# Operand preparation, product order and row ends in the late half of an encoder block

## The chip, the cores and the metric

The kernel runs on one core of one Trainium2 chip. The metric is the time of one execution on the device in microseconds. The kernel before was timed three times: 2582.22, 2582.96 and 2584.04 us, median 2582.96. One further execution was recorded by the profiler.

The core has five engines with a queue each: TensorE (PE) multiplies matrices, VectorE (DVE) and ScalarE (ACT) work elementwise, GpSimd (POOL) does little here, and SyncE (SP) issues all DMAs of this kernel, in order.

## The reference

One layer over 2048 positions of 1024 features: a mixing part (two head groups), a feed-forward part with a causal convolution, and a last norm. The part around the change is the feed-forward of the second half of the positions:

```python
def conv_ffn(h, w_up, w_conv, b_conv, w_down):
    a = h @ w_up
    C = a.shape[-1]
    a = lax.conv_general_dilated(
        a, w_conv[:, None, :].astype(a.dtype), window_strides=(1,),
        padding=[(CONV_W - 1, 0)], dimension_numbers=('NWC', 'WIO', 'NWC'),
        feature_group_count=C) + b_conv.astype(a.dtype)
    g, val = jnp.split(a, 2, axis=-1)
    return (jax.nn.silu(g) * val) @ w_down
...
        x = x + jnp.concatenate([out_a, out_b], axis=-1) @ w_out[l]
        x = x + conv_ffn(rms_norm(x, norm_ffn_g[l]), w_up[l], w_conv[l], b_conv[l], w_down[l])
    return rms_norm(x, norm_final_g)
```

`D_MODEL` is 1024, `D_FF` 2816, `CONV_W` 3. Inputs and output are float32.

## The kernel before

Every float32 product is made of three matmuls with operands in a rounded format: each operand is split into a high part (a copy by ScalarE that rounds) and a low part (the difference, by VectorE), and high x high, high x low and low x high are summed. The helper `both` (L911) makes such a pair. So every operand costs one ScalarE and one VectorE operation before TensorE can use it.

The kernel is one stream of instructions in which a planner, at build time, gives every engine its order by its own estimate of times; the order in the source is a priority, not the order of execution. Tiles come from pools; a tile has a name, and `BUFS` (L39) says how many buffers each name has. A new tile waits until an old one in its place has been read for the last time. When one pool is closed and another opened, the new tiles lie where the old ones lay.

The first half of the positions (1024) goes through mixing, up projection, convolution and down projection in other functions, which the change doesn't touch. The second half goes through `late_half` (L960):

- `c_late` (L922) ends the mixing part. It leaves rows in DRAM (`rows_d`) and normed, transposed rows in the tiles `yf`.
- **Up projection.** The 1024 rows and the 2 x 2816 columns are handled by a scheme with seven products for eight (Strassen's, in Winograd's form). The rows' operands are called Y: P1 and P2 use quarters of the rows as they are (y11, y21), P3 to P7 use sums and differences (Y22, T4, T1, T2, T3), which `first` (L983) and the lines after it build with VectorE. The columns are done in 22 chunks (`NF`) of 128 gate and 128 value columns. For each chunk f, `up_raw` (L1034) loads two weight tiles `rawl` (gate and value, 512 KB each), `up_gate` (L1041) splits the gate part for P1 and P2 (tiles xgP1, xgP2), and `up_sums` (L1047) makes and splits the five sums for P3 to P7 (tiles sf, xs). One product is 12 matmuls (`prod`, L1011), into a PSUM bank A, B or C.
- `up_step(f)` (L1067) does a chunk: it first computes P1 of the chunk f + 1 into a bank A and copies it to a tile `pc` (`kept`, L1029); adds C of f and its kept P1 into `cv` (L1081); then P6 on top of P1 (kept as u2), P7 (kept as p7), P5 on top of A, sums with p7 (L1086), P4 on top of B, sum with u2 (L1087), P3 on top of A, and copies A (L1089). Then P2 of f + 1 into a bank C, the sums of f + 1, the loads and the gate split of f + 2. The convolution, the gate and the store to `act_d[f]` follow (L1099 to L1112). A chunk of 2 x 1024 values is in `cv` (2 buffers) until its gate is formed.
- **Down projection** (`down_half`, L1114). For two blocks b of 512 rows, and for 22 chunks f of the inner dimension: load a chunk of the weights (`rawl`) and of `act_d` (`df`), split both (dh, dl, ah, al, 5 buffers each), and do 24 matmuls for four row tiles t and two column halves, accumulating in 8 PSUM banks D. The last four chunks go row by row instead (L1166): all four for t = 0, then its end, and so on. `end` (L1140) adds the row to what `rows_d` holds, squares it (the squares go to a tile that is called `df` as well), forms the norm factor by a power on GpSimd, scales and stores the row.

All DMAs are issued by SP, each in its turn: a store that waits for its data holds the loads behind it.

Of the kernel before, what the change touches and what calls it, by code (L numbers as in the profile page):

```python
# [18 lines left out]
P = 128  # L19
S = 2048  # L20
D = 1024
KC = D // P
DFF = 2816
NF = DFF // P
HALF = 1024
TB = 512
EPS = 1e-6
# [9 lines left out]


BUFS = {  # L39
    "raw": 2, "rawl": 4, "whi": 4, "wlo": 4, "thi": 1, "tlo": 1, "acc": 8,  # L40
# [7 lines left out]
}  # L48


# [4 lines left out]
class Block:  # L55
# [904 lines left out]
    def late_half(self, accp, close_c):  # L960
        nc, tc = self.nc, self.tc
        self.c_late(accp)
        close_c()
        kw = dict(bufs=1, reuse_waits="tile")
        es = ExitStack()
        self.rawp = self.ctx.enter_context(tc.tile_pool(name="rawlate", **kw))
        xp = self.xp = es.enter_context(tc.tile_pool(name="xpool", **kw))
        yp = es.enter_context(tc.tile_pool(name="y2pool", **kw))
        self.up = es.enter_context(tc.tile_pool(name="upool", **kw))
        self.upp = es.enter_context(tc.tile_pool(name="ups", space=PSUM, **kw))  # L970
        self.w_up = self.a["w_up"][0].rearrange("(c p) n -> p c n", p=P)
        self.X, self.ps, self.p1 = {}, {}, {}
# [36 lines left out]
        self.down_half(1)  # L1009
# [21 lines left out]
        self.nc.scalar.activation(t, ps, AF.Copy)  # L1031
        return t

    def up_raw(self, f):  # L1034
        self.raw = getattr(self, "raw", {})
        for c, c0 in ((0, f * P), (1, DFF + f * P)):
            t = self.til(self.rawp, [P, 1024], F32, "rawl")
            self.dma(t.rearrange("p (a b) -> p a b", b=P), self.w_up[:, :, c0:c0 + P])
            self.raw[f, c] = t

    def up_gate(self, f):  # L1041
        g = self.raw[f, 0]
# [21 lines left out]
        for n in S:  # L1064
            self.X[f, n] = S[n]

    def up_step(self, f):  # L1067

        nc = self.nc
        tt = nc.vector.tensor_tensor  # L1070
        if f:
            if f + 1 < NF:
                p1 = self.prod(f + 1, "P1", "A")
                self.p1[f + 1] = self.kept(p1)
        else:
            for i in range(2):
                self.p1[i] = self.kept(self.ps[i, "A"])
        a = self.til(self.fp, [P, 2, HALF + 2], F32, "cv")
        nc.scalar.activation(a[:, :, 0:2], self.halo[:, f:f + NF + 1:NF, :], AF.Copy)
        lo, hi = slice(2, 2 + TB), slice(2 + TB, 2 + HALF)  # L1080
        tt(a[:, 0, lo], self.ps.pop((f, "C")), self.p1.pop(f), op=ALU.add)  # L1081
        A = self.prod(f, "P6", "A")
# [6 lines left out]
        nc.scalar.activation(a[:, 0, hi], A, AF.Copy)  # L1089
        for k in ("A", "B"):  # L1090
            self.ps.pop((f, k))
        if f and f + 1 < NF:
            self.prod(f + 1, "P2", "C")
        if f + 1 < NF:
            self.up_sums(f + 1)
        if f + 2 < NF:
            self.up_raw(f + 2)
            self.up_gate(f + 2)
# [15 lines left out]
    def down_half(self, half):  # L1114

        nc, tc = self.nc, self.tc
        w_down = self.a["w_down"][0].rearrange("(f p) n -> p f n", p=P)
        with ExitStack() as es:
            kw = dict(bufs=1, reuse_waits="tile")
            dp = es.enter_context(tc.tile_pool(name="downp", **kw))  # L1120
            pp = es.enter_context(tc.tile_pool(name="downs", space=PSUM, **kw))
            gf = dp.tile([P, D], F32, name="gf")
            self.dma(gf, self.a["norm_final_g"].unsqueeze(0).broadcast_to([P, D]))
            for b in range(2):
                bank = {}
                parts = []

                def mms(f, t):
                    w, x = parts[f]
                    ts = slice(t * P, (t + 1) * P)  # L1130
                    for col in range(2):
                        cs = slice(col * 512, (col + 1) * 512)
                        if f == 0:
                            bank[t, col] = self.til(pp, [P, TB], F32, "D")
                        ps = bank[t, col]
                        for i, j in ((0, 0), (0, 1), (1, 0)):
                            nc.tensor.matmul(ps, lhsT=x[i][:, ts], rhs=w[j][:, cs], start=f == 0 and i + j == 0,  # L1137
                                             stop=f == NF - 1 and i == 1)

                def end(t):  # L1140
                    i = 4 * b + t
                    x = self.til(dp, [P, D], F32, "xo")
                    self.dma(x, self.rows_d[i])
                    for col in range(2):
                        cs = slice(col * 512, (col + 1) * 512)
                        nc.vector.tensor_tensor(x[:, cs], bank[t, col], x[:, cs], op=ALU.add)
                    junk = self.til(dp, [P, D], BF16, "df")
                    r = self.row_scale(self.fp, x, junk)
                    nc.vector.scalar_tensor_tensor(x, x, r, gf, op0=ALU.mult, op1=ALU.mult)
                    t0 = half * HALF + i * P  # L1150
                    self.dma(self.out[0, t0:t0 + P, :], x)

                for f in range(NF):
                    raw = self.til(self.rawp, [P, 1024], F32, "rawl")
                    self.dma(raw, w_down[:, f, :])
                    w = [self.til(dp, [P, 1024], F32R, "dh"), self.til(dp, [P, 1024], F32R, "dl")]
                    self.both(w, raw)
                    xf = self.til(dp, [P, TB], F32, "df")
                    self.dma(xf, self.act_d[f][:, b * TB:(b + 1) * TB])
                    x = [self.til(dp, [P, TB], F32R, "ah"), self.til(dp, [P, TB], F32R, "al")]  # L1160
                    self.both(x, xf)
                    parts.append((w, x))
                    if f < NF - 4:
                        for t in range(4):
                            mms(f, t)
                for t in range(4):  # L1166
                    for f in range(NF - 4, NF):
                        mms(f, t)
                    end(t)

    def run(self):
        tc = self.tc
# [50 lines left out]
```

## Time and profile before

| | us |
|---|---|
| median of three runs | 2582.96 |
| the profiled execution, its own time | 2580.12 |
| its span, on which all positions below lie | 2578.3 |
| up projection of the late half, first matmul | 1872.4 |
| its last product ends | 2310.4 |
| down projection, first matmul | 2316.5 |
| its first block ends | 2439.3 |
| its second block begins | 2449.3 |
| its last matmul ends | 2570.6 |

The profile gives each engine's busy time. TensorE's records are pipelined, so its busy time overstates it a little: a matmul of 0.39 us follows its predecessor by 0.23 us. A row of the timeline reads: start, length, engine, line, operation, output tile <- input tiles, shapes, count, and in brackets the idle time just before and who ended it. A row of the waits reads: who waited, for whom, us in total, times, longest. L72 is the line through which every DMA is issued, L913 and L914 are the two operations of `both`; for these the tile's name tells what is meant.

### The profile page before, as it was taken

The page shows a single profiled execution, that of the slowest core. Times are in us where ns is not written, and L with a number is a line of the kernel's source. Part 1 is how long each engine was busy: PE and PEld are TensorE (multiplying, and loading weights), DVE is VectorE, ACT ScalarE, POOL GpSimd, SP SyncE. Part 2 cuts the span into 40 slices and gives each one's busy share as a digit, 9 for nine tenths or more (in the row PEclk, how much of TensorE's full clock was granted, in tenths as well). Part 3 has the DMA queues.
Part 4 walks back from the last instruction along what each step waited for, and adds up shares of the span by engine and source line. Part 5 has one row for each costly group of instructions (what it writes and reads, how often), then busy time and mean ns, then how long its engine had stood idle before and what let it go on. Part 6 is the DMA issues. An engine that isn't in the chain of part 4 may idle for free.

```text
span 2578.3 us, 32600 instructions
## 1 busy us (share of the span) xinstructions
PE 2503.3 (97%) x11346; PEld 2048.2 (79%) x11346; DVE 1707.3 (66%) x2981; ACT 1269.4 (49%) x2376; POOL 291.3 (11%) x314
## 2 busy tenths in 40 slices
PE   8999999999999999999999999999989999999898
PEld 5787777878788888888888888887868888878687
DVE  5237676565458777777776777766388888884433
ACT  4337687554356555554545554553345455453332
POOL 3204131000112001001100100112100000000000
PEclk9999999999999999999999999999999999999999
DMA  6863524666733233323332323356413222236452
GB/s 185 256 164 92 176 90 142 171 187 210 263 120 119 88 105 112 97 87 105 108 101 87 106 93 91 110 174 228 155 49 97 75 89 82 81 112 209 158 170 71
DMA packets 314880, 336.27 MB, mean 130 GB/s; under 512 B 49596, under 2 KB 218756, under 8 KB 314700
## 3 DMA queue, kind: packets, MB, share of 16 engines
q1 hardware_dynamic: 314716, 334.19, 42.3%
q8 instruction: 90, 1.47, 0.2%
q14 instruction: 74, 0.61, 0.1%
HBM read 267.80 MB, written 66.46 MB: 130 GB/s over the span
## 4 chain that ended last, share of the span: by engine, by line
PE 85%; DMA 4%; DVE 4%; ACT 3%; issue 2%; POOL 1%; SPq 0%; POOLq 0%; ACTq 0%; DVEq 0%
PE mm L174 12%; PE mm L172 12%; PE mm L176 12%; PE D L1137 9%; PE dn L172 3%; PE dn L174 3%; PE dn L176 3%; PE A L1026 3%; PE A L1025 3%; PE A L1024 3%; PE s L656 2%; PE s L716 2%; PE o L705 2%; PE s L655 2%; PE s L717 2%; PE o L704 2%
## 5 line engine op out<-in xcount | busy, mean ns | idle before, releaser
L172 PE MATMUL mm<-thi,whi 128*128 128x512 f32 x960 | 376.3, 392 | 1.9 <-DVE vn L381 1.9
L174 PE MATMUL mm<-tlo,whi 128*128 128x512 f32 x960 | 376.6, 392 | 0.0
L176 PE MATMUL mm<-thi,wlo 128*128 128x512 f32 x960 | 376.3, 392 | 0.2 <-DVE wlo L126 0.2
L664 ACT ACTIVATE s<-s,part 128x512 f32<-128x512 f32 (+3 forms) x320 | 190.6, 596 | 214.0 <-DVE part L659 138.4
L728 DVE TENSOR_TENSOR pl<-e,ph 128x512 fp32r<-128x512 f32 (+1 forms) x320 | 204.7, 644 | 111.4 <-PE o L705 67.3
L172 PE MATMUL mm<-whi,thi 128*128 128x512 f32 x640 | 253.9, 399 | 7.2 <-POOL whi L114 5.5
L174 PE MATMUL mm<-wlo,thi 128*128 128x512 f32 x640 | 254.5, 398 | 3.1 <-DVE wlo L126 3.0
L176 PE MATMUL mm<-whi,tlo 128*128 128x512 f32 x640 | 252.8, 395 | 0.0
L722 ACT ACTIVATE e<-s 128x512 f32<-128x512 f32 (+1 forms) x320 | 166.6, 531 | 174.6 <-PE s L717 84.2
L727 ACT ACTIVATE ph<-e 128x512 fp32r<-128x512 f32 (+1 forms) x320 | 179.2, 567 | 131.9 <-PE o L704 118.0
L114 POOL TENSOR_SCALAR whi<-raw 128x1024 fp32r<-128x1024 f32 x130 | 149.1, 1149 | 796.8 <-PE mm L176 184.5
L172 PEld LDWEIGHTS mm<-thi,whi 128*128 128x128 f32 x960 | 180.4, 188 | 40.4 <-DVE vn L381 2.5
L174 PEld LDWEIGHTS mm<-tlo,whi 128*128 128x128 f32 x960 | 180.5, 188 | 37.8
L176 PEld LDWEIGHTS mm<-thi,wlo 128*128 128x128 f32 x960 | 180.4, 188 | 37.7 <-DVE wlo L126 0.7
L126 DVE TENSOR_TENSOR wlo<-raw,whi 128x1024 fp32r<-128x1024 f32 x130 | 163.8, 1262 | 60.5 <-POOL whi L114 60.4
L659 DVE TENSOR_REDUCE part<-s 128x1 f32<-128x512 f32 x192 | 127.9, 684 | 46.4 <-PE s L656 45.4
L1137 PE MATMUL D<-dh,ah 128*128 128x512 f32 x352 | 139.8, 397 | 16.0 <-ACT ah L913 16.0
L850 DVE TENSOR_TENSOR acc<-dn,acc 128x512 f32<-128x512 f32 x176 | 120.7, 686 | 52.0 <-PE dn L176 51.0
L172 PEld LDWEIGHTS mm<-whi,thi 128*128 128x128 f32 x640 | 120.9, 189 | 32.7 <-POOL whi L114 7.0
L174 PEld LDWEIGHTS mm<-wlo,thi 128*128 128x128 f32 x640 | 121.5, 190 | 29.6 <-DVE wlo L126 6.6
L176 PEld LDWEIGHTS mm<-whi,tlo 128*128 128x128 f32 x640 | 121.3, 190 | 24.0
L1137 PE MATMUL D<-dl,ah 128*128 128x512 f32 x352 | 139.3, 396 | 0.0
(295 smaller groups left out, 5506.2 us busy)
## 6 DMA issues: line engine op xcount, KB each, us to landing
m<-kx SPq DMA_DIRECT2D x160, 256.0 KB
raw<-in_w_up_dram SPq DMA_DIRECT2D x44, 512.0 KB
rawl<-in_w_up_dram SPq DMA_DIRECT2D x44, 512.0 KB
rawl<-in_w_down_dram SPq DMA_DIRECT2D x44, 512.0 KB
m<-kx SPq DMA_DIRECT2D x160, 136.0 KB
raw<-in_w_in_dram SPq DMA_DIRECT2D x40, 512.0 KB
v<-vd SPq DMA_DIRECT2D x80, 256.0 KB
x<-in_x_dram SPq DMA_DIRECT2D x24, 512.0 KB
```

Source lines behind the costliest of these rows:

```text
L114: self.cast_ins = self.nc.gpsimd.tensor_scalar(out, in_, 1.0, 0.0, ALU.mult, ALU.add).ins
L126: nc.vector.tensor_tensor(lo, raw, f32(hi), op=ALU.subtract)
L172: mm(ps, lhsT=ah[k], rhs=bh[k], start=k == 0, stop=False)
L174: mm(ps, lhsT=ah[k], rhs=bl[k], start=False, stop=False)
L176: mm(ps, lhsT=al[k], rhs=bh[k], start=False, stop=k == n - 1)
L659: nc.vector.tensor_reduce(dst, ps, axis=AX.X, op=ALU.min)
L664: nc.scalar.activation(ps[:, :n], ps[:, :n], AF.Exp, scale=-1.0, bias=dst, accum_out=ls[:, tt, sb:sb + 1])
L722: nc.scalar.activation(e[:, c], ps[:, c], AF.Exp, scale=-1.0)
L727: nc.scalar.activation(ph[:, c], e[:, c], AF.Copy)
L728: nc.vector.tensor_tensor(pl[:, c], e[:, c], f32(ph[:, c]), op=ALU.subtract)
L850: nc.vector.tensor_tensor(ac, ps, ac, op=ALU.add)
L1137: nc.tensor.matmul(ps, lhsT=x[i][:, ts], rhs=w[j][:, cs], start=f == 0 and i + j == 0, stop=f == NF - 1 and i == 1)
```

## The change

The change touches the late half only. In the up projection:

- Weight tiles: three `rawl` buffers instead of four. Gate and value parts are loaded by separate calls.
- P1 and P2 run two chunks ahead instead of one. Chunks 0, 1 and 2 have theirs emitted before the steps; the gate splits of 0 and 1 come before the sums of chunk 0, that of 2 before the transforms of the rows (`first`). xgP1 has two buffers, bank B one instead of two, bank C three instead of two.
- `up_step` is cut in `up_mms` (products) and `up_conv` (convolution, gate, store). The convolution of the last chunk is emitted after the first two preparations of the down projection.

In the down projection:

- The 44 chunks of both blocks are numbered through. `prep(n)` makes the operands of one; `ready(n + 2)` is called ahead of chunk n's matmuls, and `ready(n + 4 + max(0, t - 1))` ahead of the row tile t in the last four chunks, so chunks 0 and 1 of the second block are prepared within the last rows of the first. The operands have seven buffers.
- A row ends in two column halves: the eight times three matmuls are ordered by half, and each half is added, squared (into its own tile `jk`), scaled and stored on its own; the two sums of squares are added by one more small operation.

```diff
-    "raw": 2, "rawl": 4, "whi": 4, "wlo": 4, "thi": 1, "tlo": 1, "acc": 8,
+    "raw": 2, "rawl": 3, "whi": 4, "wlo": 4, "thi": 1, "tlo": 1, "acc": 8,
...
-    "xgP1l": 1, "xgP1h": 1,   "pc": 3, "A": 3, "B": 2, "C": 2,
-    "dh": 5, "dl": 5, "df": 3, "ah": 5, "al": 5, "xo": 4, "D": 8,
+    "xgP1l": 2, "xgP1h": 2,   "pc": 3, "A": 3, "B": 1, "C": 3,
+    "dh": 7, "dl": 7, "df": 3, "ah": 7, "al": 7, "xo": 4, "jk": 2, "s2": 2, "D": 8,
...
-        self.up_raw(0)
+        for c in range(2):
+            self.up_raw(0, c)
         self.up_gate(0)
+        self.up_gate(1)
         self.prod(0, "P1", "A")
         self.prod(0, "P2", "C")
         self.up_sums(0)
+        self.up_raw(1, 1)
+        self.up_gate(2)
...
         first(slice(384, 512))
-        self.up_raw(1)
-        self.up_gate(1)
         self.prod(1, "P1", "A")
         self.prod(1, "P2", "C")
         self.both(T3, y12)
...
         self.both(T4, y21)
+        self.prod(2, "P1", "A")
+        self.prod(2, "P2", "C")
         for f in range(NF):
-            self.up_step(f)
+            self.up_mms(f)
+            if f + 1 < NF:
+                self.up_conv(f)
         es.close()
...
+    def up_mms(self, f):
...
+        n = f + 2
+        if f == 0:
+            for i in range(3):
                 self.p1[i] = self.kept(self.ps[i, "A"])
+        elif n < NF:
+            self.p1[n] = self.kept(self.prod(n, "P1", "A"))
...
+        if f and n < NF:
+            self.prod(n, "P2", "C")
         if f + 1 < NF:
             self.up_sums(f + 1)
         if f + 2 < NF:
+            self.up_raw(f + 2, 1)
+        if f + 3 < NF:
+            self.up_gate(f + 3)
...
+            def prep(n):
+                b, f = divmod(n, NF)
+                raw = self.til(self.rawp, [P, 1024], F32, "rawl")
+                self.dma(raw, w_down[:, f, :])
+                w = [self.til(dp, [P, 1024], F32R, "dh"), self.til(dp, [P, 1024], F32R, "dl")]
+                self.both(w, raw)
+                xf = self.til(dp, [P, TB], F32, "df")
+                self.dma(xf, self.act_d[f][:, b * TB:(b + 1) * TB])
+                x = [self.til(dp, [P, TB], F32R, "ah"), self.til(dp, [P, TB], F32R, "al")]
+                self.both(x, xf)
+                parts[n] = w, x
...
+            def ready(n):
+                while len(parts) <= min(n, 2 * NF - 1):
+                    prep(len(parts))
+
+            ready(1)
+            self.up_conv(NF - 1)
             for b in range(2):
                 bank = {}
+                rows = []
+                for n in range(b * NF, (b + 1) * NF - 4):
+                    ready(n + 2)
+                    for t in range(4):
+                        mms(bank, n, t)
+                for t in range(4):
+                    ready(n + 4 + max(0, t - 1))
                     i = 4 * b + t
                     x = self.til(dp, [P, D], F32, "xo")
                     self.dma(x, self.rows_d[i])
+                    ss = self.til(dp, [P, 2], F32, "s2")
+                    jk = self.til(dp, [P, D], BF16, "jk")
                     for col in range(2):
                         cs = slice(col * 512, (col + 1) * 512)
+                        for m in range(n + 1, n + 5):
+                            mms(bank, m, t, (col,))
                         nc.vector.tensor_tensor(x[:, cs], bank[t, col], x[:, cs], op=ALU.add)
+                        nc.scalar.activation(jk[:, cs], x[:, cs], AF.Square, accum_out=ss[:, col:col + 1])
+                    rs = self.til(dp, [P, 1], F32, "rs")
+                    nc.vector.tensor_tensor(rs, ss[:, 0:1], ss[:, 1:2], op=ALU.add)
+                    nc.vector.tensor_scalar(rs, rs, 1.0 / D, EPS, ALU.mult, ALU.add)
+                    r = self.til(dp, [P, 1], F32, "rstd")
+                    nc.gpsimd.tensor_tensor(r, rs, self.mhalf[:, 0:1], op=ALU.pow)
                     t0 = half * HALF + i * P
+                    for col in range(2):
+                        cs = slice(col * 512, (col + 1) * 512)
+                        nc.vector.scalar_tensor_tensor(x[:, cs], x[:, cs], r, gf[:, cs], op0=ALU.mult, op1=ALU.mult)
+                        self.dma(self.out[0, t0:t0 + P, cs], x[:, cs])
```

The `BUFS` lines are shortened to the names that change or are spoken of. `mms` is the old function of that name with the column half as an argument.

More of the change, by code (lines that the diff above doesn't have):

```diff
@@ L971, in late_half @@
         self.w_up = self.a["w_up"][0].rearrange("(c p) n -> p c n", p=P)
-        self.X, self.ps, self.p1 = {}, {}, {}
+        self.X, self.ps, self.p1, self.raw = {}, {}, {}, {}
         (y11, y21), (y12, y22) = self.yf
@@ L1032, in kept, with up_raw @@
         return t
[L1034 to L1039, printed above, removed]
+    def up_raw(self, f, c):
+        t = self.raw[f, c] = self.til(self.rawp, [P, 1024], F32, "rawl")
+        c0 = c * DFF + f * P
+        self.dma(t.rearrange("p (a b) -> p a b", b=P), self.w_up[:, :, c0:c0 + P])
     def up_gate(self, f):
+        if f:
+            self.up_raw(f, 0)
         g = self.raw[f, 0]
@@ L1065, in up_sums @@
             self.X[f, n] = S[n]
-    def up_step(self, f):
+    def up_mms(self, f):
         nc = self.nc
         tt = nc.vector.tensor_tensor
[L1071 to L1076, printed above, removed]
+        n = f + 2
+        if f == 0:
+            for i in range(3):
                 self.p1[i] = self.kept(self.ps[i, "A"])
-        a = self.til(self.fp, [P, 2, HALF + 2], F32, "cv")
+        elif n < NF:
+            self.p1[n] = self.kept(self.prod(n, "P1", "A"))
+        a = self.cv = self.til(self.fp, [P, 2, HALF + 2], F32, "cv")
         nc.scalar.activation(a[:, :, 0:2], self.halo[:, f:f + NF + 1:NF, :], AF.Copy)
@@ L1091, in up_step @@
             self.ps.pop((f, k))
-        if f and f + 1 < NF:
-            self.prod(f + 1, "P2", "C")
+        if f and n < NF:
+            self.prod(n, "P2", "C")
         if f + 1 < NF:
@@ L1096, in up_step, with up_conv @@
         if f + 2 < NF:
-            self.up_raw(f + 2)
-            self.up_gate(f + 2)
+            self.up_raw(f + 2, 1)
+        if f + 3 < NF:
+            self.up_gate(f + 3)
+    def up_conv(self, f):
+        nc = self.nc
+        tt = nc.vector.tensor_tensor
+        a = self.cv
         t = self.til(self.fp, [P, 2, HALF], F32, "ts")
@@ L1123, in down_half @@
             self.dma(gf, self.a["norm_final_g"].unsqueeze(0).broadcast_to([P, D]))
+            parts = {}
+            def prep(n):
[9 more added lines that the diff above has]
+                parts[n] = w, x
@@ new lines, in mms @@
+            def mms(bank, n, t, cols=(0, 1)):
+                w, x = parts[n]
+                f = n % NF
+                ts = slice(t * P, (t + 1) * P)
+                for col in cols:
+                    cs = slice(col * 512, (col + 1) * 512)
+                    if f == 0:
+                        bank[t, col] = self.til(pp, [P, TB], F32, "D")
+                    for i, j in ((0, 0), (0, 1), (1, 0)):
+                        nc.tensor.matmul(bank[t, col], lhsT=x[i][:, ts], rhs=w[j][:, cs], start=f == 0 and i + j == 0,
+                                         stop=f == NF - 1 and i == 1)
@@ L1124, in down_half @@
+            def ready(n):
[3 more added lines that the diff above has]
+            self.up_conv(NF - 1)
             for b in range(2):
                 bank = {}
[L1126 to L1138, printed above, removed]
@@ L1140, in end @@
-                def end(t):
+                rows = []
[5 more added lines that the diff above has]
+                    ready(n + 4 + max(0, t - 1))
                     i = 4 * b + t
@@ L1148, in end @@
-                    r = self.row_scale(self.fp, x, junk)
-                    nc.vector.scalar_tensor_tensor(x, x, r, gf, op0=ALU.mult, op1=ALU.mult)
-                    t0 = half * HALF + i * P
[L1151 to L1169, printed above, removed]
+                        nc.scalar.activation(jk[:, cs], x[:, cs], AF.Square, accum_out=ss[:, col:col + 1])
[3 more added lines that the diff above has]
+                    r = self.til(dp, [P, 1], F32, "rstd")
```

2 lines of the change are left out of this document (1 added, 1 removed), and 2 rows, old and new, of the table BUFS.

## The prediction

> **What bounds the kernel now.** The page comes first, then a table by stage of the part that the change touches (the list of stages, with busy time and granted clock), then the waits of TensorE in that part.
>
> ```profile
> span 2578.3 us, 32600 instructions
> PE 2503.3 (97%) x11346; PEld 2048.2 (79%) x11346; DVE 1707.3 (66%) x2981; ACT 1269.4 (49%) x2376; POOL 291.3 (11%) x314
> ...
> 1872.40:1923.70 51.30, 42.69 (x171) 33.41 (x170) 43.98 (x53) 23.96 (x33) 0.93 (x1) 0.90 0.15 42
> 1923.70:2310.40 386.70, 386.70 (x1690) 316.41 (x1688) 326.74 (x400) 197.12 (x299) 0.00 (x0) 1.00 0.25 82
> 2310.40:2316.50 6.10, 0.01 (x1) 0.00 (x0) 6.06 (x6) 6.03 (x7) 0.00 (x0) 0.66 0.93 300
> 2316.50:2439.30 122.80, 122.77 (x528) 101.08 (x528) 52.89 (x60) 39.02 (x50) 1.65 (x3) 0.98 0.53 179
> 2439.30:2449.30 10.00, 0.08 (x2) 0.04 (x1) 5.94 (x8) 2.83 (x4) 0.55 (x1) 0.64 0.94 322
> 2449.30:2570.60 121.30, 121.30 (x528) 100.04 (x528) 45.05 (x52) 32.99 (x44) 1.65 (x3) 0.99 0.37 121
> 2570.60:2578.30 7.70, 0.04 (x1) 0.00 (x0) 2.21 (x4) 1.15 (x2) 0.55 (x1) 0.80 0.27 112
> ...
> PE D L1137 <- ACT ah L913: 16.0, 2, 9.9
> PE A L1026 <- DVE xgP1l L914: 4.1, 1, 4.1
> PE B L1025 <- DVE t3l L914: 3.9, 1, 3.9
> ...
> 2569.57 0.39 PE L1137 MATMUL D<-dh,al 128*128 128x512 f32 x1
> ...
> 2570.25 0.39 PE L1137 MATMUL D<-dh,al 128*128 128x512 f32 x1
> ```
>
> The columns of a stage are its length, busy time of PE, PEld, DVE, ACT and POOL with counts, the granted clock, the DMA share and GB/s. TensorE bounds the kernel: nothing but fewer or shorter holes in it pays. The last two rows lie three matmuls apart, 0.68 us, so one takes 0.2267 us. That prices the holes:
>
> - Entry of the up projection (1872.4 to 1923.7). Its 171 records are 163 products' matmuls, 37.0 us, and two sets of short transposes, about 1.2. So 51.3 less 38.2, 13.1 us, is lost.
> - The steady up projection (next row) has no hole.
> - Entry of the down projection: 6.1 us of nothing, and 122.8 us for 528 matmuls that need 119.7. So 6.1 + 3.1 = 9.2 us. The extra is a reduced clock: 0.66 granted in the hole.
> - The border of the two row blocks: 10.0 us, then 121.3 for 119.7, together 11.6.
> - The tail: 7.7 us behind the last matmul.
>
> The change has 41.6 us before it, 1.6% of the span; it adds no matmul and takes none away.
>
> **Part 1: three product pairs first (entry of up).** Who is late here is read from the timelines of VectorE and ScalarE.
>
> ```profile
> 1883.07 0.68 DVE L914 TENSOR_TENSOR xgP1l<-rawl,xgP1h 128x512 fp32r<-128x512 f32 x1
> ...
> 1888.71 0.69 DVE L914 TENSOR_TENSOR xgP1l<-rawl,xgP1h 128x512 fp32r<-128x512 f32 x1 [1.95 <-ACT xgP1h L913]
> ...
> 1897.22 2.28 DVE L914 TENSOR_TENSOR t3l<-cv,t3h 128x2048 fp32r<-128x2048 f32 x1
> ...
> 1905.70 0.68 DVE L914 TENSOR_TENSOR t2l<-cv,t2h 128x512 fp32r<-128x512 f32 x1
> ...
> 1888.05 0.63 ACT L913 ACTIVATE xgP1h<-rawl 128x512 fp32r<-128x512 f32 x1 [8.83 <-PE A L1025]
> ```
>
> VectorE is busy 43.98 of 51.3 us here and its early part is nearly solid: it makes T3 (ready 1899.5) and T2 (ready 1906.4), without which P7 and P6 of step 0 cannot run. TensorE's first wait, 4.1 us, is for the low part of chunk 1's gate weights, at 1883.07. The chain then turns on itself: xgP1 has one buffer, so ScalarE sits 8.83 us until TensorE has read it, and VectorE 1.95 us behind ScalarE. The new order makes the gate parts of chunks 0 and 1 at once, with two xgP1 buffers, and all six leading products (72 matmuls, 16.3 us) can run before T3. That moves one product, 2.7 us, into the time that is lost anyway, and takes VectorE's 1.95 us of idle out of the way of T3 and T2. Against it stand chunk 2's two splits (2 x 0.68 on VectorE) ahead of T3, and the fact that P2 of chunk 2 no longer fills the wait for T2.
>
> If T3 and T2 come no earlier, step 0 ends where it does, and I bound the part at a loss of 0.5 us; if they come 3 us earlier, at a gain of 5. I take +2.5, near the idle that goes. The 13.1 us are thus mostly kept: they are VectorE's.
>
> **Part 2: the steady steps.** Weight buffers (rawl 4 to 3), one B bank for two, and P1 and P2 two chunks ahead change the ring of every step. Nothing is gained (no hole), so the question is what it costs.
>
> ```profile
> 2089.93 0.58 ACT L1089 ACTIVATE cv<-A 128x512 f32<-128x512 f32 x1
> ...
> 2098.91 0.21 ACT L1079 ACTIVATE cv<-halo 128x4 f32<-128x4 f32 x1 [1.29 <-DVE ts L1110]
> ...
> 2118.15 0.21 ACT L1079 ACTIVATE cv<-halo 128x4 f32<-128x4 f32 x1 [1.29 <-DVE ts L1110]
> ...
> 2100.05 0.69 DVE L1081 TENSOR_TENSOR cv<-C,pc 128x512 f32<-128x512 f32 x1
> ```
>
> A step takes 19.24 us (the two halo copies). The tightest new ring is pc, which keeps three buffers: P1's copies of two coming steps and u2 hold all three, so p7's copy now waits until L1081 of the following step has used its own P1 copy. That needs a cv buffer, free when the step before has been convolved. In the rows: from L1089 (2089.93) to the end of L1081 (2100.74) 10.8 us; then p7's copy 0.6 (as L1089), L1086 0.7 (as L1081), twelve matmuls of P3 2.7, and about 0.6 for hand-overs (an estimate from the 0.1 to 0.3 between neighbouring rows): 15.4 us a turn against 19.24. The other four products and the two early ones fill the waiting. The weight loads have one buffer less, but P1 and P2 of a chunk can stand anywhere in their step. I take 0, from +1 down to -15 if the ring bites.
>
> **Part 3: entry of down, conv of the last chunk put behind two preparations.**
>
> ```profile
> 2300.79 0.58 ACT L1089 ACTIVATE cv<-A 128x512 f32<-128x512 f32 x1
> ...
> 2309.58 0.33 SPq L72 DMA_DIRECT2D act<-ts  x1
> 2309.96 0.42 SPq L72 DMA_DIRECT2D gf<-in_norm_final_g_dram  x1
> 2310.45 0.60 ACT L1089 ACTIVATE cv<-A 128x512 f32<-128x512 f32 x1 [0.75 <-PE A L1026]
> 2310.47 1.71 SPq L72 DMA_DIRECT2D df<-act  x3
> 2310.94 1.99 ACT L913 ACTIVATE dh<-rawl 128x1024 fp32r<-128x1024 f32 x2
> ...
> 2315.86 1.29 ACT L913 ACTIVATE ah<-df 128x512 fp32r<-128x512 f32 x2
> ```
>
> ScalarE was idle 0.75 us ahead of 2310.45 and yet no dh was made before: the weights' parts stand behind the last L1089 in its queue, as if the pool of the down projection opens only there. Its first ah comes after four dh copies (4 x 1.05) and a conv operation. On SP, the df loads stand behind the store of chunk 20, which waits for that chunk's convolution: 0.83 us before the end of the last product. DMA then runs at 300 GB/s with a share of 0.93, so the first df cannot land much earlier than it is issued.
>
> The edit keeps the place of the pool, so the late dh stays. It shortens the queue ahead of ah (two preparations, three weight buffers) by one or two dh, 1.05 to 2.1 us, and the conv operation, 1.2. And chunk 20's store may come earlier against the end: the last two steps now have no P1 or P2 to run, five products of 12 (13.6 us) against the 9.66 us between the two L1089, if they are not interleaved as now. I take 2.0 us of the 9.2: lower bound 0 (the landing decides), upper 9.2 (all ready at the end, and no slow matmul). The conv behind the two preparations costs nothing beside TensorE's 10.9 us for chunks 0 and 1; its store is read only with the last chunk of block 0.
>
> **Part 4: the border.**
>
> ```profile
> 2442.42 1.78 SPq L72 DMA_DIRECT2D df<-act  x3
> ...
> 2448.58 0.63 ACT L913 ACTIVATE ah<-df 128x512 fp32r<-128x512 f32 x1 [4.72 <-DMA df<-act]
> ...
> 2449.26 0.79 PE L1137 MATMUL D<-dh,ah 128*128 128x512 f32 x1 [9.92 <-ACT ah L913]
> ```
>
> Here the cause is plain. The last four chunks hold four of five operand buffers, and the squares of the row ends use df's three, so the next block's df loads are issued 3.1 us after TensorE stopped and land in a burst (322 GB/s, share 0.94). With seven buffers, squares in tiles of their own, and chunks 22 and 23 prepared beside rows 2 and 3 of block 0, these loads have 10.9 us of matmuls above them. Work beside them: two preparations take VectorE 2 x (1.22 + 0.69) = 3.8 us, two row ends about 3.0 each, 9.8 of 10.9 us; it just fits, and is spread as the chunks may be made earlier. So the whole 11.6 us less a little: +11.4, down to +6 if df is still late by a part of the burst.
>
> **Part 5: rows in two parts (tail).** From the timelines at the end and SP's waits:
>
> ```profile
> 2571.46 1.06 ACT L137 ACTIVATE df<-xo 128x1024 bf16<-128x1024 f32 x1 [4.29 <-DVE xo L1146]
> ...
> 2573.46 1.28 DVE L1149 SCALAR_TENSOR_TENSOR xo<-xo,rstd,gf 128x1024 f32<-128x1024 f32 x1 [0.66 <-POOL rstd L141]
> ...
> SPq L1219 <- DMA out_dram<-xo: 2.1, 1, 2.1
> ```
>
> Behind the last matmul a half square replaces the whole: 1.06 less about 0.6 (a 128x512 operation, as L1089), 0.45 gained; one more small addition costs 0.15 to 0.2. The two halves of the last product take as long as the whole, but the first half is stored 0.65 us sooner, and the last store is 256 KB. At 300 GB/s that is 0.87 us less to move. I take 0.6 of it, bounds 0 and 0.9. So +0.9 (0.3 to 1.4).
>
> The Trainium skill, "DMA: Bandwidth & Descriptors", section "Anatomy of one DMA", speaks against this: some 2.0 us of a DMA is fixed, mostly the write's receipt, and only the rest scales with bytes. By it nearly all of the 2.1 us above would stay, and the sum would be 0.4 us smaller; no row here has a store of 256 KB alone to tell.
>
> **Sum:** 2.5 + 0 + 2.0 + 11.4 + 0.9 = 16.8 us. The profiled execution took 2580.1 us, 1.8 around its span; the median of the runs shown is 2582.96. As a difference it carries over: 2583.0 - 16.8 = **2566 us**.
>
> **Rivals.**
>
> *The entry of down closes too.* If df and dh of the first two chunks are made before the last product ends (their old neighbours in memory are read early in that step), all 9.2 us go, 7.2 more than in my sum: **2559**. For it: df's loads need only stand ahead of or right behind chunk 20's store. Against it: the late dh. Here the Trainium skill, "TensorE: Matmul & The Clock Gate", section "Part 1: The HAM clock gate", gives a half-way case: an idle window of about 3.4 us halves the clock. By it a hole cut from 6.1 to under 3.4 us would also save the 3.1 us of slow matmuls, one of 4.1 us would not; the trace agrees so far as waits of 3.9 us and more are followed by slow ones.
>
> *The border keeps a part.* The loads of chunks 22 and 23, output stores and residual rows share one SP queue in order; a store that waits for a row's end holds the df behind it. Half of the 11.4 us stays: **2572**.
>
> *The step ring becomes the bound (slower).* Place: p7's copy in each step. It decides when a turn of that ring exceeds 19.24 us, 3.8 us more than my 15.4. VectorE is busy 326.74 of 386.70 us, so L1081 can be queued behind others: behind the eight 0.69 us operations of a step's sums and splits it is 5.5 us later, a turn of 20.9, 1.7 us for each of 19 steps, 32 us lost against 16.8 won: **2598**. Break-even is 0.9 us a step. Against it: TensorE has other products to run and the order around it is free.
>
> *It doesn't do what it says:* the order of the queues comes out so that the two entries lose 5 us and the border keeps half: 2583.0 + 5 - 5.7 - 0.9, **2581**, no change.
>
> **How the numbers follow.** Forecast (2561 to 2571) 0.55; entry closed 0.17; border half kept 0.10; ring 0.08 slower than 2588 and 0.04 between; nothing 0.06. A measurement of this kernel can tell about 0.2%, 5.2 us: faster means under 2577.8, 0.84; within 0.2% 0.08; slower 0.08. For 8 in 10 the range takes the forecast, most of the closed entry and the half-kept border: 2556 to 2575.
>
> **What would show it.** Border: no wait of L1137 on ah, matmuls 0.227 us apart across it. Entry of down: a shorter wait there, L1089 still ahead of dh. Entry of up: six leading products without the 4.1 us wait, then one longer wait for t3l. Steady: halo copies 19.24 us apart; 20 or more would make the ring right and the forecast wrong. Tail: about 6.8 us. A wait at the border of over 3 us, or a step over 20 us, would refute it.

## The result, and the profile after

The changed kernel took 2616.15 us (median of 4, 2613.9 to 2620.15) beside 2583.5 us for the kernel before (4, 2582.22 to 2585.19): a ratio of 1.0128, 95% interval 1.011 to 1.0145. It is slower by 33 us; 2566 was predicted, with 2575 as the upper end.

Line numbers of the changed kernel differ from those of before: products L1030 to L1032, `kept` L1037, the halo copy L1085, the copy of A to `cv` L1095, the convolution L1116 (ScalarE), L1117 and L1118 (VectorE), its tanh L1122, the products of the down projection L1160, the last scaling L1197.

The list of stages of the profiled execution (span 2613.2 us), same columns as before (length; busy time of PE, PEld, DVE, ACT, POOL; granted clock, DMA share, GB/s), shows where to look:

```profile
1926.80:2358.00 431.20, 399.49 (x1679) 319.15 (x1678) 322.11 (x396) 191.43 (x297) 0.00 (x0) 0.98 0.22 72
2358.00:2364.50 6.50, 0.04 (x2) 0.02 (x1) 6.46 (x7) 5.21 (x7) 0.00 (x0) 0.82 0.98 292
2364.50:2490.00 125.50, 125.50 (x544) 103.74 (x545) 61.35 (x76) 47.31 (x69) 1.65 (x3) 0.98 0.59 203
2490.00:2605.50 115.50, 115.50 (x511) 95.65 (x511) 43.05 (x57) 29.91 (x47) 2.58 (x4) 1.00 0.39 130
```

The steady up projection, which had no hole (386.70 us busy of 386.70), now has TensorE busy 399.49 of 431.20 us. The hole ahead of the down projection is still there. Behind it PE is busy throughout, across the border too. TensorE's waits from 1860 us on name what holds it:

```profile
PE A L1030 <- ACT pc L1037: 30.3, 18, 2.0
PE D L1160 <- ACT ah L913: 6.5, 1, 6.5
...
PE B L1030 <- ACT pc L1037: 1.4, 2, 0.8
```

Twenty waits for a `pc` copy, 31.7 us, one a step and none over 2.0 us, are new. The border's wait of 9.92 us is gone. The halo copies of three steps give the pace:

```profile
2018.78 0.20 ACT L1085 ACTIVATE cv<-halo 128x4 f32<-128x4 f32 x1
...
2040.21 0.20 ACT L1085 ACTIVATE cv<-halo 128x4 f32<-128x4 f32 x1
...
2062.48 0.20 ACT L1085 ACTIVATE cv<-halo 128x4 f32<-128x4 f32 x1
```

21.43 and 22.27 us a step, for 19.24 before. The balance, after less before: the up projection takes 484.9 us (1873.1 to 2358.0) for 438.0, +46.9; it starts 0.7 later; the down projection takes 248.26 (to its last matmul's end at 2606.28) for 260.23, -12.0; the tail 6.92 for 7.66, -0.7. Together +34.9, the difference of the spans. So the down projection and the tail brought 12.7 us of the 14.3 that were forecast for them, and the up projection took that back nearly four times.

**What a step waits for.** The timeline of TensorE, with the ends of two P6 and of P1, and then P5:

```profile
2002.93 0.39 PE L1032 MATMUL A<-t2h,xsP6l 128*128 128x512 f32 x1
...
2023.83 0.39 PE L1032 MATMUL A<-t2h,xsP6l 128*128 128x512 f32 x1
...
2037.59 0.40 PE L1032 MATMUL A<-y11h,xgP1l 128*128 128x512 f32 x1
2039.86 0.51 PE L1030 MATMUL A<-t1h,xsP5h 128*128 128x512 f32 x1 [1.87 <-ACT pc L1037]
...
2041.36 0.63 PE L1030 MATMUL A<-t1h,xsP5h 128*128 128x512 f32 x1
...
2044.77 0.39 PE L1032 MATMUL A<-t2h,xsP6l 128*128 128x512 f32 x1
```

And ScalarE's queue at the same place:

```profile
2037.78 1.06 ACT L1122 ACTIVATE cv<-ts 128x1024 f32<-128x1024 f32 x1 [4.01 <-DVE ts L1118]
2038.74 1.07 ACT L1037 ACTIVATE pc<-A 128x512 f32<-128x512 f32 x2
```

P5 is summed on top of the P6 of its chunk, in the same bank A, so it may start only when that P6 has been copied (u2). Counted from the first product on, TensorE runs P6 nearly two steps ahead of P5 here: the P5 at 2039.86 is that of chunk 6, whose P6 was done at 2003.3; the P6 that ends at 2024.2 is already that of chunk 7. The copy that P5 waits for begins at about 2039.2, 36 us after its P6 was done: it is the second of the "x2" row, behind the copy of an early P1 (that of chunk 8), with which it shares the ring `pc`, and both stand behind the tanh of the convolution. In this order P1 is the last product of the step (its last matmul starts at 2037.59), and nothing is left to run between it and P5. In the steps where TensorE goes on with P6, as at 2018.46, that product waits for the first of the two copies, since it is summed on top of the P1 that has just ended.

The tanh is late because the convolution is, and the chain of waits shows the whole turn (start, length, what):

```profile
2000.68 0.69 DVE cv L1092
...
2002.00 0.70 DVE sf L1064
2002.73 0.70 DVE sf L1066
2003.48 3.74 DMA rawl<-in_w_up_dram
...
2007.78 0.62 ACT xgP2h L913
2008.40 1.14 ACT ts L1116
...
2013.25 1.20 DVE ts L1117
...
2015.05 1.21 DVE ts L1118
2016.34 1.06 ACT cv L1122
...
2017.92 0.49 ACT pc L1037
2018.46 0.50 PE A L1030
```

It starts with the sum behind P5 (L1092). The sums of the next chunk follow and end the use of a weight buffer; the load of the next gate weights goes into it, 3.74 us; ScalarE's splits xgP1 and xgP2 wait at the head of its queue, with the convolution behind them; then convolution, tanh, copies, P5 (from 2019.03; the row at 2018.46 is the P6 just ahead of it), and L1092 again at 2022.06. That is a turn of 21.4 us, just the step. It is a ring, as the prediction's rival said, but not over p7's copy.

### The profile page after: what moved, and what is told of

It reads as the page before. It is cut to its first block, busy times and chain, and to the rows that moved or that the text cites. A ratio compares the mean times of both kernels' runs of the same rounds, so it can differ in the third digit from the quotient of the medians.

```text
span 2613.2 us, 32595 instructions
## 1 busy us (share of the span) xinstructions
PE 2515.4 (96%) x11346; PEld 2049.6 (78%) x11346; DVE 1707.1 (65%) x2997; ACT 1268.6 (49%) x2392; POOL 291.4 (11%) x314
## 4 chain that ended last, share of the span: by engine, by line
PE 75%; DVE 8%; DMA 6%; ACT 6%; issue 3%; POOL 1%; SPq 0%; DVEq 0%; POOLq 0%; ACTq 0%
PE mm L172 12%; PE mm L174 12%; PE mm L176 12%; PE D L1160 9%; PE dn L172 3%; PE dn L176 3%; PE dn L174 3%; DMA rawl<-in_w_up_dram 2%; PE s L716 2%; PE s L717 2%; PE s L656 2%; PE o L705 2%; PE o L704 2%; PE s L655 2%; PE A L1030 2%
## 5 line engine op out<-in xcount | busy, mean ns | idle before, releaser
L1160 PE MATMUL D<-dh,ah 128*128 128x512 f32 x352 | 138.4, 393 | 6.5 <-ACT ah L913 6.5
L172 PE MATMUL dn<-whi,ar 128*128 128x512 f32 x352 | 138.2, 393 | 0.0
```

The source lines that it names most:

```text
L172: mm(ps, lhsT=ah[k], rhs=bh[k], start=k == 0, stop=False)
L1160: nc.tensor.matmul(bank[t, col], lhsT=x[i][:, ts], rhs=w[j][:, cs], start=f == 0 and i + j == 0, stop=f == NF - 1 and i == 1)
```

## The experiments

Two theories at first: the **ring** above is the loss, or the scarce **weight buffers and banks** as such. The expectations name parts of the ring: "loop theory" is the whole turn with the load in it, "order theory" u2's place behind P1's copy, "ring theory" the three `pc` buffers alone, whatever the loads do, "slot theory" that three such buffers are too few in any order. In the edits the lines of `BUFS` are cut to the names that change.

**1 and 2: each half of the change alone.** The up projection of before with the down projection of after, and the reverse. Of the first run's edit against the kernel before, some lines:

```diff
-    "dh": 5, "dl": 5, "ah": 5, "al": 5,
+    "dh": 7, "dl": 7, "ah": 7, "al": 7, "jk": 2, "s2": 2,
...
+            ready(1)
+            self.up_conv(NF - 1)
```

> The up projection of the kernel before (its steps, loads, banks and buffers), with the down projection of the changed one (two chunks ahead, rows in two parts, the last convolution behind two preparations). If the whole loss sits in the up projection's steps: the up projection takes 438 us again, the down projection 248 and the tail 6.9, so about 2571 us, ratio 0.995. If the down projection's gain was only lent by the later up projection, 2583.

> The changed up projection with the down projection of before. If the parts simply add: 2616 + 12 + 0.8 = about 2629 us, with the 10 us wait at the border of the blocks back and the waits of about 1.7 us in each step kept. If the down projection's operands, put into the same memory, cause the steps' waits: about 2583 or less.

Measured: 2570.86 us, ratio 0.9951 (0.9936 to 0.9966), and 2635.93 us, ratio 1.0203 (1.0187 to 1.0218). The longest wait of TensorE in the first, which has none for a copy:

```profile
PE D L1155 <- ACT ah L913: 6.5, 1, 6.5
```

and in the second:

```profile
PE A L1029 <- ACT pc L1036: 32.3, 18, 2.2
PE D L1149 <- ACT ah L913: 16.6, 2, 10.1
```

The up projection holds all of the loss: 2570.86 less 2583.5 is -12.6, 2635.93 less 2583.5 is +52.4, and their sum, 39.8, is near the +32.7 of both (the second came out 7 us higher than expected). The border's wait, 10.1 us, is there with the old down projection and not with the new.

**3 and 4: the ring `pc`.** One buffer more, or a ring of its own for P1's copies.

```diff
-    "pc": 3,
+    "pc": 4,
```

> The changed kernel with four pc buffers instead of three, nothing else. Order theory (u2's copy stands behind the copy of P1 of two chunks ahead in the same ring of tiles, in order, so P5 waits until that P1 is done): the order stays, the waits stay, 2610 to 2620 us. Slot theory (the prediction's rival: three buffers are too few, and p7's copy waits for the sum that frees one): the steps fall to 19.3 us, about 2572.

```diff
-    "pc": 3,
+    "pc": 2, "pk": 2,
...
-    def kept(self, ps):
-        t = self.til(self.up, [P, TB], F32, "pc")
+    def kept(self, ps, tag="pc"):
+        t = self.til(self.up, [P, TB], F32, tag)
...
-            self.p1[n] = self.kept(self.prod(n, "P1", "A"))
+            self.p1[n] = self.kept(self.prod(n, "P1", "A"), "pk")
```

> The changed kernel with the copies of P1 in tiles of their own (pk, two buffers) and pc with two for u2 and p7: as many buffers as with four pc, but u2 no longer follows P1 in one ring. Order theory: no wait of P5 on u2, steps of 19.1 to 19.4 us, about 2570 us. Slot theory: the same as four pc buffers in one ring. If the weights' late loads ahead of the convolution in ScalarE's queue are the cause: steps of 20 us or more, 2590 to 2616.

Measured: 2580.28 us, 0.9995 (0.9986 to 1.0005), which fits neither end; and 2570.03 us, 0.995 (0.9934 to 0.9967), as the order theory said, with one wait for a copy left, 0.5 us. The four-buffer run is the instructive one. Its waits for copies into A, then ScalarE's queue in two neighbouring steps, with TensorE's first row behind P1 in the second:

```profile
PE A L1030 <- ACT pc L1037: 9.6, 9, 1.3
```

```profile
2049.56 1.06 ACT L1122 ACTIVATE cv<-ts 128x1024 f32<-128x1024 f32 x1 [2.69 <-DVE ts L1118]
...
2051.05 1.07 ACT L1037 ACTIVATE pc<-A 128x512 f32<-128x512 f32 x2
...
2068.71 0.39 PE L1032 MATMUL C<-y21h,xgP2l 128*128 128x512 f32 x1
2068.91 1.09 ACT L1037 ACTIVATE pc<-A 128x512 f32<-128x512 f32 x2 [2.86 <-PE A L1032]
...
2070.36 1.07 ACT L1122 ACTIVATE cv<-ts 128x1024 f32<-128x1024 f32 x1
```

Nine waits for eighteen: in every other step the planner put the copies ahead of the tanh, and TensorE waits only in the steps where they stand behind it. In the steps without a wait TensorE has another order too: ten matmuls of P2 stand behind P1, and the copies run under them. So the number of buffers alone does not decide; the order of instructions on ScalarE and TensorE does, which is written at build time.

**5, 6 and 7: three other links of the ring.** A fourth weight buffer (for which xgP1 goes back to one); two banks B (for which C goes back to two); and P1's copy emitted behind p7's.

```diff
-    "rawl": 3,  "xgP1l": 2, "xgP1h": 2,
+    "rawl": 4,  "xgP1l": 1, "xgP1h": 1,
```

> The changed kernel with four weight buffers (rawl) again, and, to make room, one xgP1 buffer; three pc buffers as changed. Loop theory (each step turns in one loop: P5, its sum, the sum that frees a weight buffer, the load of 3.7 us, the gate split at the head of ScalarE's queue, the convolution behind it, u2's copy behind that, P5 again): the load drops out of the loop, steps of 19.2 to 20 us, 2570 to 2585 us. Ring theory (the pc ring alone holds P5, whatever the loads do): the waits stay near 1.7 us a step, 2605 to 2620.

```diff
-    "B": 1, "C": 3,
+    "B": 2, "C": 2,
```

> The changed kernel with two banks B and two C as before. Loop theory and ring theory: bank B isn't in the loop, 2610 to 2620 us. Bank theory (P7 of the next step can't start beside P4 of this one, so TensorE has nothing to run while it waits): waits mostly gone, 2570 to 2585.

```diff
-        elif n < NF:
-            self.p1[n] = self.kept(self.prod(n, "P1", "A"))
...
         p7 = self.kept(self.prod(f, "P7", "B"))
...
+        if f and n < NF:
+            self.p1[n] = self.kept(self.prod(n, "P1", "A"))
```

> The changed kernel with P1 of two chunks ahead emitted behind u2's and p7's copies of its step, not ahead of them; three pc buffers in one ring, three weight buffers, one bank B, all as changed. Loop theory and ring theory: u2's copy no longer follows P1's copy, P5 is ready when wanted, steps of 19.1 to 19.4 us, 2568 to 2573 us, as with two rings but with no memory more. Slot theory (three pc buffers are too few in any order): p7's copy still waits for the sum of the next step, 2580 or more.

Measured: 2572.68 us, 0.996 (0.9944 to 0.9976); 2567.12 us, 0.9937 (0.9917 to 0.9956); 2567.75 us, 0.994 (0.9925 to 0.9955). The fifth and the seventh came as the loop theory said; the fifth goes against the `pc` ring alone, which was to give 2605 to 2620, and the seventh against too few `pc` buffers (2580 or more). In the fifth the whole of P2 stands behind P1, so the planner's order changed with the buffers, and the run doesn't isolate the load. The sixth was a miss for the loop theory, which held the second bank B to be no part of it and expected 2610 to 2620; the bank theory (2570 to 2585) had the sign. But the fourth, the fifth and the seventh run have one bank B and hardly a wait, so one bank alone is not the loss. ScalarE's queue with two banks B:

```profile
2045.03 1.09 ACT L1037 ACTIVATE pc<-A 128x512 f32<-128x512 f32 x2 [3.41 <-PE A L1032]
...
2046.52 1.06 ACT L1122 ACTIVATE cv<-ts 128x1024 f32<-128x1024 f32 x1
```

Here too the copies stand ahead of the tanh. They wait for P1 (3.41 us) and run as soon as it ends, while TensorE still has ten matmuls of P2 to do. That run did not show why the planner orders it so with one bank more; only that it does. With P1 emitted late, the copy of u2 (first row) goes ahead of the tanh by itself, and the wait for the weights' load harms nothing. The timeline of ScalarE and its waits between 1930 and 2280 us:

```profile
2057.23 0.58 ACT L1037 ACTIVATE pc<-A 128x512 f32<-128x512 f32 x1
...
2060.02 1.06 ACT L1122 ACTIVATE cv<-ts 128x1024 f32<-128x1024 f32 x1 [1.21 <-DVE ts L1118]
```

```profile
ACT xgP1h L913 <- DMA rawl<-in_w_up_dram: 58.5, 18, 4.1
```

ScalarE waits 58.5 us for loads, three times as much as in the changed kernel (17.4 in the same stretch), and TensorE has no wait in that stretch. A late load is a loss only if something that TensorE needs stands behind it.

**8: gf's load later.** With the seventh run as base, the load of the final norm's weights is emitted at the end of block 0.

```diff
-            self.dma(gf, self.a["norm_final_g"].unsqueeze(0).broadcast_to([P, D]))
...
+                if b == 0:
+                    self.dma(gf, self.a["norm_final_g"].unsqueeze(0).broadcast_to([P, D]))
```

> As the one before, and the last norm's weights (gf, 512 KB) loaded within block 0 of the down projection, so that the first three loads of df stand right behind the last but one store. Landing theory (the first wait of the down projection is the time in which DMA at 290 to 300 GB/s moves what was issued ahead of df): 0.5 MB less ahead of it, 1.7 us, so a wait of about 3.5 us instead of 5.2 and 1.5 to 3 us off the time. Queue theory (ScalarE's dh copies and the convolution ahead of ah decide): no change.

Measured: 2567.71 us, 0.994 (0.9924 to 0.9957), no change, as the queue theory said, and the first wait of the down projection stays at 5.2 us. ScalarE works there without a pause, so this run alone can't tell whether the load came sooner.

**9: both cures.** The seventh edit with the sixth's banks.

```diff
-    "B": 1, "C": 3,
+    "B": 2, "C": 2,
```

> The kernel after with both cures at once: two banks B (and two C), and P1 of chunk f + 2 emitted behind the copy of P7. If both open the same loop, they don't add: no step waits, steps of 19.1 to 19.3 us, 2564 to 2568 us, like each alone (2567.1 and 2567.8). If each leaves a rest of its own in the steps, the sum is better by more than 3 us: below 2564.

Measured: 2568.18 us, 0.994 (0.9928 to 0.9953). They don't add: the ring is open or it is not.

**10: the scarce buffers without the early P1.** Run 1 with two names cut.

```diff
-    "rawl": 4,  "B": 2,
+    "rawl": 3,  "B": 1,
```

> The up projection of before with the down projection of after (2570.9 us), and in it only the two cuts in buffers: three rawl buffers for four and one bank B for two. P1 stays one chunk ahead, with its copy where it was. Loop theory: the scarce buffers alone don't close the loop, since only one copy of P1 stands in the ring of three pc; no step waits of 1 us or more, 2568 to 2577 us. Buffer theory: the scarce buffers are the cost, whatever is ahead; waits of 1.3 to 2.0 us in most steps, above 2600 us.

Measured: 2568.58 us, 0.9943 (0.9929 to 0.9956). Its steady stage:

```profile
1926.80:2310.00 383.20, 383.20 (x1675) 314.01 (x1674) 322.47 (x397) 197.56 (x297) 0.00 (x0) 1.00 0.25 81
```

TensorE is busy 383.20 of 383.20 us. The buffer theory, which expected over 2600 us, falls: one weight buffer and one bank less cost nothing while P1 is one chunk ahead.

**11 and 12: what holds the entry of the down projection.** On the kernel of run 9, GpSimd makes the high parts of the rows of chunks 0 and 1; then gf's load is moved as in run 8 too.

```diff
-                self.both(x, xf)
+                if n < 2:
+                    self.cast(x[0], xf)
+                    self.nc.vector.tensor_tensor(x[1], xf, f32(x[0]), op=ALU.subtract)
+                else:
+                    self.both(x, xf)
```

> As the run with both cures, but the high parts of the rows of down chunks 0 and 1 are made by GpSimd (0.71 us for 128x512 in another place of the trace) in place of ScalarE, whose queue holds three dh copies and an operation of the convolution ahead of them. Queue theory: the first wait of the down projection falls from 5.2 to between 2.5 and 3.7 us, and the time by 1.5 to 4 us against the run with both cures. Landing theory: the loads of the rows land hardly before 2315, the wait stays at 4.7 us or more, and the time within 1 us.

> As the run with the high parts on GpSimd, and the load of the final norm's weights (gf, 512 KB) goes behind the first three loads of rows in SP's order. In the run before, GpSimd had nothing to do and took the first rows 5.9 us after their load was issued, behind the store of a chunk and gf, 512 KB each. Bytes theory: what stands ahead sets the landing; without gf it comes 1.2 to 1.8 us sooner, 4.1 to 4.7 us after the issue, the first wait of the down projection falls from 7.1 to 5.3 to 5.9 us, and the time by 1 to 2 us. Receipt theory: the load waits for the store's end or for a time that doesn't depend on bytes ahead; it lands 5.5 to 6.1 us after the issue as before, and the time stays within 1 us.

Measured: 2568.74 us, 0.9946 (0.9933 to 0.996), and 2567.3 us, 0.9937 (0.9923 to 0.995). The load and its first reader in the one, where GpSimd had nothing else to do:

```profile
2309.59 1.76 SPq L72 DMA_DIRECT2D df<-act  x3
...
2315.51 1.65 POOL L114 TENSOR_SCALAR ah<-df 128x512 fp32r<-128x512 f32 x2 [439.40 <-DMA df<-act]
```

and in the other:

```profile
2306.46 1.78 SPq L72 DMA_DIRECT2D df<-act  x3
...
2310.51 1.66 POOL L114 TENSOR_SCALAR ah<-df 128x512 fp32r<-128x512 f32 x2 [437.39 <-DMA df<-act]
...
2311.64 2.93 PE L1163 MATMUL D<-dh,ah 128*128 128x512 f32 x6 [4.73 <-POOL ah L114]
```

The first rows are there 5.9 us after their issue with gf's 512 KB ahead, 4.05 without: the bytes ahead set the landing, by 1.9 us. TensorE's wait goes from 7.1 to 4.7 us. Taking ScalarE out alone gained nothing (the wait was 6.4 us in run 9). In run 9 ScalarE stood idle for 1.1 us until the rows came, 5.7 us after their issue; in run 8, where only gf was moved, ScalarE came to the rows 6.4 us after the issue and found them there. So two things end here about 1 us apart, ScalarE's queue and the landing, and either one moved alone leaves the other. In the times the 1.4 us between the two runs can't be told from nothing.

Runs 6 to 12, 2567.1 to 2568.7 us, are faster than both kernels and not to be told apart; the plainest is the sixth, two names in `BUFS`.

## Why the prediction was wrong, point by point

**Part 2, the steady steps: here it failed.** It was taken at 0, with 15 us as the worst; it cost 46.9 us (the entry's share of the up projection hardly changed, see part 1). Two sentences carry the error: "P1 and P2 of a chunk can stand anywhere in their step", and "The other four products and the two early ones fill the waiting". P1 came last in the step, with P2 already done, and no product was left. The planner put it there, although its operands (the low part ends at 2030.0) and its bank (the copy out of it ends at 2032.0) were there before P2 began; why it did is not shown:

```profile
2029.34 0.69 DVE L914 TENSOR_TENSOR xgP1l<-rawl,xgP1h 128x512 fp32r<-128x512 f32 x1 [1.07 <-ACT xgP1h L913]
...
2031.39 0.58 ACT L1095 ACTIVATE cv<-A 128x512 f32<-128x512 f32 x1
...
2032.22 0.39 PE L1030 MATMUL C<-y21h,xgP2h 128*128 128x512 f32 x1
```

And the prediction looked only at the third copy in the ring, p7's (15.4 us a turn). The second, u2's, is the one that TensorE waits for, since P5 is summed in the bank that it must read first. The prediction counted the order of tiles in `pc`, but not the order of instructions on ScalarE: a copy behind the split that waits for a load, and behind the tanh.

Of the 46.9 us, 31.7 are waits. Another 12 or so are matmuls that follow each other more slowly than by 0.2267 us behind a wait, mostly by 0.43 us; the rest is not attributed.

**The rival "the step ring becomes the bound"** was right in its sign, its kind and nearly its price (2598, 1.7 us a step; it was 2616, 2.2 to 3.0 a step) and wrong in its place. It got 0.12 between its two cases. Its sign of refutation, "a step over 20 us", is what the trace shows. The rivals of a closed entry and of a half-kept border did not come: the entry's wait is still there, and the border's is gone.

**Part 1, entry of up: +2.5 was too much.** TensorE's idle in that stage is 8.46 us after and 8.61 before. T3's low part is ready 25.5 us after the first matmul for 27.1 before, as hoped, but TensorE had run out by then as long before. What slow matmuls add is 4.4 us before and 4.5 after, but 3.0 and 2.1 in runs 7 and 6, which keep the new entry (idle 8.48 and 8.79). So, by one trace each, it is worth nothing here and 1.5 to 2.1 us there.

**Part 3, entry of down: 2.0 did not come.** The timeline of ScalarE after, and TensorE's first row:

```profile
2358.55 2.94 ACT L913 ACTIVATE dh<-rawl 128x1024 fp32r<-128x1024 f32 x3
2361.38 1.23 ACT L1116 ACTIVATE ts<-cv,colB 128x1024 f32<-128x1024 f32 x1
2363.80 1.97 ACT L913 ACTIVATE ah<-df 128x512 fp32r<-128x512 f32 x3 [1.18 <-DMA df<-act]
...
2364.48 0.79 PE L1160 MATMUL D<-dh,ah 128*128 128x512 f32 x1 [6.46 <-ACT ah L913]
```

The late dh stayed, as predicted. The operation of the convolution is still ahead of ah, though it is emitted behind the preparations: the planner decides, not the source. The queue did get shorter, and then ah waits 1.18 us for its load. The wait is 6.46 us for 6.12; with 0.7 us less of slow matmuls the stage gained 0.4. The lower bound, "0 (the landing decides)", was the case, and runs 11 and 12 show it.

**Part 4, the border: right.** +11.4 was predicted; no wait of L1160 stands there, and the down projection's 12.0 us less the 0.4 of its entry leave 11.6.

**Part 5, the tail: right.** +0.9 was predicted, 0.7 came. The halves behind the last product:

```profile
2607.04 0.63 ACT L1188 ACTIVATE jk<-xo 128x512 bf16<-128x512 f32 x1 [0.84 <-DVE xo L1187]
...
2608.80 1.42 DVE L1197 SCALAR_TENSOR_TENSOR xo<-xo,rstd,gf 128x512 f32<-128x512 f32 x2 [0.66 <-POOL rstd L1193]
```

The square takes 0.63 us for 1.06. From the end of the scaling (2610.22) to the end of the span are 3.0 us, before it was 3.6 (2574.74 to 2578.3): the 0.6 that the prediction took for the smaller store. The prediction took it from the rule of the Trainium skill ("DMA: Bandwidth & Descriptors", "Anatomy of one DMA") that the sum would be 0.4 us smaller; that was a misreading. By the rate that the Trainium skill gives in that section for the part that scales with bytes, 436 GB/s, 256 KB less are 0.6 us less, an estimate, and the trace agrees. That section is about DMAs that GpSimd issues, though, and these are issued by SP.

Without the ring, the sum was nearly right: with it open (run 7) the change takes 2567.75 us, 15.75 less than before, where 16.8 was the sum. Parts 1 and 3 are still the short ones there: about 1.5 for 2.5, and 1.0 for 2.0 (a wait of 5.2 us for 6.1).

## What to carry to other kernels

When work is made earlier, follow each of its instructions into every in-order queue that it passes, and ask which older result shares a ring or a queue place behind it: here an early product's copy held back a copy whose product had been done for 36 us. A planner's order is part of the change: with other buffer counts, copies went ahead of a tanh or behind it, and one product ahead of another or behind it, so compare the order on each engine, not only the tiles. A step without holes has no slack to be seen in TensorE's row; the slack to look for is how many matmuls stand between a result and the next product that needs it.

## What was not expected of the hardware

Short waits cost more than their length. After the wait of 1.87 us above, eight rows from 2041.36 on are some 0.63 us long and 0.43 apart, up to 2044.77, and the granted clock between 2039.9 and 2044.2 is 0.67:

```profile
2039.90:2044.20 4.30, 4.30 (x13) 3.45 (x14) 2.61 (x4) 1.59 (x4) 0.00 (x0) 0.67 0.30 122
```

Eight times 0.2 us, 1.6 us, nearly doubles that wait. Of the twenty waits in the steps, six of 1.83 to 2.04 us are followed by such a stretch of some 3.4 us (here 2041.36 to 2044.77). Two others as long, 2.00 us (1953.37) and 1.91 us (2083.60), are not, nor are the twelve from 0.69 to 1.67 us. So the length of a wait alone does not tell, and what else decides is open. The Trainium skill, "TensorE: Matmul & The Clock Gate", section "Part 1: The HAM clock gate", states an idle window of about 3.4 us before the clock is halved. The trace does not agree: 1.83 us was enough here.
